# Constants generated in eight pieces, own keys by differences of values, heads' result split two at a time, gates loaded one pair ahead

## The chip, the core and the metric

The kernel runs on one core of a Trainium2 chip. The time is that of one launch on the device, in microseconds (us): the median of the runs of a version. The core's engines run side by side, each from its own queue of instructions in order, and wait for one another by semaphores: TensorE (PE in the profile, with its weight loads as PEld), VectorE (DVE), ScalarE (ACT), GpSimd (POOL) and SyncE (SP), which here issues the loads from device memory. Matmuls write to PSUM banks; DVE and ACT read them out.

## The reference

Two layers, each a mixer of sliding-window attention and a gated linear recurrence (HGRN2), merged by sigmoid gates, over 1024 tokens of width 1024, all in float32:

```python
for layer in range(DEPTH):                       # DEPTH 2
    h = rms_norm(x, norm_w[layer])
    q, k, v, z_attn, q_h, f_h, i_h, g_h, gate_attn, gate_hgrn = split(h @ w_in[layer])
    a = sliding_window_attention(rope(q), rope(k), v, sinks) * silu(z_attn)   # 8 heads of 64, 2 kv heads, window 128
    o = hgrn2_recurrence(silu(q_h), (1 - lb) * sigmoid(-f_h), i_h, log(lb + (1 - lb) * sigmoid(f_h)))
    b = rms(o) * hgrn_norm_w[layer] * silu(g_h)                                # 4 heads of 128
    x = x + (sigmoid(gate_attn) * (a @ w_up_attn[layer])
             + sigmoid(gate_hgrn) * (b @ w_up_hgrn[layer])) @ w_out[layer]
return rms_norm(x, final_norm_w)
```

A query attends to the keys of its own block of 128 up to itself and to those of the block before that lie in the window. `lb` comes from `lb_logits` by a softmax over the layers; rotary embedding needs the cosine and sine of position times frequency. These, some masks and `hnw` (`hgrn_norm_w`) are the kernel's constants.

## The kernel before

Each float32 product is three matmuls of rounded parts (`proj3`: high x high, high x low, low x high). A weight chunk is loaded raw (`wr`), its high part is cast by ACT (`whi` or `wh`, L128) and its low part is a subtraction on DVE (`wlo` or `wl`, L129). The raw chunks share two buffers, so a load starts only when the chunk two before it has been split. All SBUF slots, PSUM banks and buffers come from pools; a planner sets the order on each engine by priorities from the order of the code and by when buffers and inputs are free. SyncE takes the loads in its own order: one that waits for a buffer holds up the rest.

A layer goes through these stages:

- **Input projection of gates, q, k and v by pairs** (`pair_first`, `pair_rest`, 13 pairs): a pair of 128 columns goes through sums of weight blocks (`ws`, L277 to L281), split into `whi_s`/`wlo_s` and `whi_t`/`wlo_t` and half a chunk split into `wh`/`wl` (L285, L286), and five groups of 12 matmuls into the banks `pb` and `pc` (L291 to L293). DVE adds a bank to earlier parts (`pq`, L303), which frees it; ACT applies the sigmoid and sends the gate to memory (`gd`).
- **Constants** (layer 0): `constants()` runs whole behind pair 1. It loads the masks, makes `lb` and `oml`, the angles `ang` (L407, eight multiplications), their reduction (`nrn`, L410 to L423) and two sines (L426, L427). ACT holds one table of functions at a time, so the sines cost a load (L426) and a load back to the sigmoid's (L473). `tables()` behind pair 5 makes four tables `tab` of cosine and sine (memset by POOL, L436; DVE, L439 to L443), turns each by four PE transposes (`tt`, L447) and stores it.
- **z, attention, values**: attention runs block by block (8 blocks), with projections between. `scores` puts own keys and those of the block before into one tile of 128 columns (a column is either the one or the other), `softmax` makes `pr`, `turn` transposes it (`tp`, L721) and DVE multiplies it twice from PSUM (L724): by the mask of past keys, `side[:, 0]`, into `pT[:, 0]` and by that of own keys into `pT[:, 1]`. `values` (L733) multiplies these by the values `vn` of the block before and of its own into `av`.
- **HGRN heads**: `core(h)` for four heads in a stagger of 25 steps, with `filling()` between: the heads' projections, then `up_attn` (`pu_ua`; its result `u1` is copied by ACT, L800, and multiplied by the gate `ga`, L825). `finish_head` transposes a head's result (`tb`, L1020) and DVE writes it to half of `b` (L1021); `b` has two halves of the tokens (`a`) and two pairs of heads. Behind the last head, `split_act` casts the four parts on ACT (`b0h`, `b1h` in layers 0 and 1, L781) and subtracts on DVE (`b0l`, `b1l`, L782).
- **Up projection of HGRN**: for each pair `m` of eight column blocks `up_chunk` loads weights (`wr_uh`), `gate_in` loads two gates `u2` (shown as `u<-gd`, L806), PE makes `pu_uh`, DVE multiplies by the gate in place (L802), adds `u1` (L1080), and ACT and DVE split the sum into `mg` (L1082, L1083).
- **Output projection** with `w_out` (`wr_o`, `po`), and in layer 0 the loads of `x` for the next norm.

Of the kernel before, what the change touches and what calls it, by code (L numbers as in the profile page):

```python
# [10 lines left out]
F32 = mybir.dt.float32  # L11
# [27 lines left out]
def trunk_kernel(ctx, tc, x, positions, norm_w, w_in, attn_sinks, hgrn_norm_w, w_up_attn,  # L39
# [313 lines left out]

    tabs = [dp.tile([P, T], F32, name=f"tabs_{i}") for i in range(2)]

    def constants():

        ones = cp.tile([P, 32], F32, name="ones")
        G.memset(ones, 1.0)
        side = cp.tile([P, 2, P], F32, name="side")  # L360
        nc.sync.dma_start(side, c_side)
        upper = cp.tile([P, P], I32, name="upper")
        nc.sync.dma_start(upper, c_upper)
        never = cp.tile([P, 1], F32, name="never")
        G.memset(never, -1e30)
        mdiag = cp.tile([P, 32], F32, name="mdiag")
        nc.sync.dma_start(mdiag, c_diag)
        mlev = cp.tile([P, NLEV, 32], I32, name="mlev")
        nc.sync.dma_start(mlev, c_lev)
        freq = cp.tile([P, HALF], F32, name="freq")  # L370
        nc.sync.dma_start(freq, c_freq)
        posi = cp.tile([P, NB], I32, name="posi")
        nc.sync.dma_start(posi, positions.rearrange("o (b p) -> p (o b)", p=P))
        sink = cp.tile([P, DEPTH, NH], F32, name="sink")
        nc.sync.dma_start(sink, attn_sinks.rearrange("(o l) h -> o l h", o=1).broadcast_to([P, DEPTH, NH]))
        hnw = cp.tile([P, DEPTH], F32, name="hnw")
        nc.sync.dma_start(hnw, hgrn_norm_w.rearrange("l p -> p l"))
        lbl = cp.tile([P, DEPTH, NHG], F32, name="lbl")
        nc.sync.dma_start(lbl, lb_logits.rearrange("l (h p) -> p l h", p=P))


        lbm = cp.tile([P, NHG], F32, name="lbm")
        tc.keep_in_program_order(V.tensor_tensor(out=lbm, in0=lbl[:, 0], in1=lbl[:, 1], op=ALU.max))
        lbe = cp.tile([P, DEPTH, NHG], F32, name="lbe")
        for l in range(DEPTH):
            V.tensor_tensor(out=lbe[:, l], in0=lbl[:, l], in1=lbm, op=ALU.subtract)
        S.activation(lbe, lbe, AF.Exp)
        lbs = cp.tile([P, NHG], F32, name="lbs")
        V.tensor_tensor(out=lbs, in0=lbe[:, 0], in1=lbe[:, 1], op=ALU.add)
        V.reciprocal(lbs, lbs)  # L390
        lsm = cp.tile([P, DEPTH, NHG], F32, name="lsm")
        for l in range(DEPTH):
            V.tensor_tensor(out=lsm[:, l], in0=lbe[:, l], in1=lbs, op=ALU.mult)
        lb = cp.tile([P, DEPTH, NHG], F32, name="lb")
        V.tensor_tensor(out=lb[:, 0], in0=lsm[:, 0], in1=lsm[:, 0], op=ALU.subtract)
        lbc = cp.tile([P, NHG], F32, name="lbc")
        V.tensor_tensor(out=lbc, in0=lsm[:, 0], in1=lsm[:, 1], op=ALU.add)
        V.tensor_tensor(out=lb[:, 1], in0=lbc, in1=lsm[:, 0], op=ALU.subtract)
        oml = cp.tile([P, DEPTH, NHG], F32, name="oml")
        V.tensor_scalar(out=oml, in0=lb, scalar1=-1.0, scalar2=1.0, op0=ALU.mult, op1=ALU.add)  # L400


        posf = cp.tile([P, NB], F32, name="posf")
        tc.keep_in_program_order(V.tensor_copy(posf, posi))
        ang = cp.tile([P, NB, HALF], F32, name="ang")
        for b in range(NB):
            V.tensor_scalar(out=ang[:, b], in0=freq, scalar1=posf[:, b:b + 1], scalar2=None, op0=ALU.mult)  # L407
        nrn = cp.tile([P, NB, HALF], F32, name="nrn")
        big = 1.5 * 2.0 ** 23
        V.tensor_scalar(out=nrn, in0=ang, scalar1=1.0 / (2.0 * math.pi), scalar2=None, op0=ALU.mult)  # L410
        V.tensor_scalar(out=nrn, in0=nrn, scalar1=big, scalar2=None, op0=ALU.add)
        V.tensor_scalar(out=nrn, in0=nrn, scalar1=-big, scalar2=None, op0=ALU.add)
        rest = 2.0 * math.pi
        for bits in (2, 8, 8, 24):
            if bits == 24:
                c = float(np.float32(rest))
            else:
                e = math.floor(math.log2(rest))
                q = 2.0 ** (e - (7 if bits == 8 else 7))
                c = math.floor(rest / q) * q  # L420
            V.scalar_tensor_tensor(out=ang, in0=nrn, scalar=-c, in1=ang, op0=ALU.mult, op1=ALU.add)
            rest -= c
        V.tensor_scalar(out=ang, in0=ang, scalar1=3.1415925, scalar2=-3.1415925, op0=ALU.min, op1=ALU.max)  # L423
        sins = cp.tile([P, NB, HALF], F32, name="sins")

        S.activation(sins, ang, AF.Sin)  # L426
        S.activation(nrn, ang, AF.Sin, scale=0.5)  # L427
        V.tensor_tensor(out=nrn, in0=nrn, in1=nrn, op=ALU.mult)
        return ones, side, upper, never, mdiag, mlev, sink, hnw, lb, oml, sins, nrn

    def tables(sins, nrn):
        for i in range(2):
            for g in range(2):
                b = slice(4 * g, 4 * g + 4)
                t = hp.tile([P, 4, P], F32, tag="po", name=f"tab_{i}_{g}")
                G.memset(t, 1.0 - i)  # L436
# [19 lines left out]
    def first_chunk(L, m, slots):  # L456

        nm = f"p{L}_{m}"
        return (split_slot if slots else split_w)(load_chunk(w_in[L], pairs[m][0][0], nm), nm, [P, KT, P])


    for L in range(DEPTH):
# [135 lines left out]
        for m in range(NPAIR):  # L598
# [8 lines left out]
                    S.activation(tr[r][:, t0:t0 + 512], o[key], AF.Copy, scale=qkv[r][1])  # L607
            if m == 12:
                cosT, sinT = rotary()
            if L == 0 and m == 1:  # L610
                ones, side, upper, never, mdiag, mlev, sink, hnw, lb, oml, *angles = constants()
            elif L == 0 and m == 5:
                tables(*angles)
        for i, (part, nm) in enumerate(((hT.hi, "hi"), (hT.lo, "lo"))):
            for j in range(2):
                part[1][j] = slot([P, 2, 512], f"h{nm}_{L}_{j}", F32R)
# [25 lines left out]
        def z(j, w, groups):  # L642
# [4 lines left out]
                nc.scalar.dma_start(zd[:, j, t], d)  # L647
            colsA(w[0], w[1], hT, f"z{L}_{j}", use, groups)

        w = [chunk(wi, OZ + j * P, f"z{L}_{j}") for j in range(2)]  # L650
        stack(0)
        stack(1)
# [12 lines left out]
        z(2, w[2], [H0, H1])  # L665
        stack(5)
        z(3, w[3], [H0, H1])


        probs = {}  # L670
# [43 lines left out]
        def turn(b):  # L714
            pr, _ = probs[b]
            probs[b] = []
            for g in range(2):

                tp = bank([P, 2, 2, P], f"tp_{L}_{b}_{g}")
                for j in range(4):  # L720
                    PE.transpose(tp[:, j % 2, j // 2], pr[:, 4 * g + j], ident)  # L721
                pT = slot([P, 2, 4, P], f"pT_{L}_{b}_{g}")
                for pt in ([0, 1] if b else [1]):
                    V.tensor_tensor(out=pT[:, pt], in0=tp.rearrange("p r i q -> p (r i) q"),  # L724
                                    in1=side[:, pt].unsqueeze(1).broadcast_to([P, 4, P]), op=ALU.mult)
                probs[b].append(pT)

        def values(b):
            av = bank([P, 4, P], f"av_{L}_{b}")
            for g, pT in enumerate(probs.pop(b)):  # L730
                for pt in ([0, 1] if b else [1]):
                    for r in range(2):
                        PE.matmul(av[r * HD:(r + 1) * HD, 2 * g:2 * g + 2].rearrange("p h q -> p (h q)"),  # L733
                                  lhsT=vn[0][:, b if pt else b - 1, g * HD:(g + 1) * HD],
                                  rhs=pT[:, pt, 2 * r:2 * r + 2].rearrange("p h q -> p (h q)"),
                                  start=pt == 0 or b == 0, stop=pt == 1)
            d = hp.tile([P, 4, P], F32, tag="po", name=f"avo_{L}_{b}")
# [31 lines left out]
        for u in range(4):  # L769
            before(NB + u)  # L770
            (forget if u < 2 else query)(0, w[u // 2], [(H0, H1)[u % 2]])
            attend(NB + u)

        def split_act(src, nm):
            res = []
            for a in range(2):
                row = []
                for j in range(2):
                    hi = slot([P, 2, 512], f"{nm}h_{a}_{j}", F32R)
                    lo = slot([P, 2, 512], f"{nm}l_{a}_{j}", F32R)  # L780
                    S.copy(hi, src[a][j])  # L781
                    V.tensor_tensor(out=lo, in0=src[a][j], in1=hi.bitcast(F32), op=ALU.subtract)  # L782
                    row.append((hi, lo))
                res.append(row)
            return res


        def up_chunk(w, m, nm):
# [38 lines left out]


        bt = [[None] * 2 for _ in range(2)]

        scTs = [slot([P, NB, P], f"scT_{L}_{i}") for i in range(2)]
        for t in scTs:
# [2 lines left out]
        def core(h):  # L835
# [176 lines left out]
            def finish_head():  # L1012
                gs = slot([P, T], f"gg_{nm}")
                nc.sync.dma_start(gs, gd[(2 * KT + h) * P:(2 * KT + h + 1) * P])
                for a in range(2):
# [3 lines left out]
                    for j in range(4):  # L1019
                        PE.transpose(tp[:, j], ot[:, 4 * a + j], ident)  # L1020
                    V.scalar_tensor_tensor(out=bt[a][h // 2][:, h % 2], in0=tp.rearrange("p j q -> p (j q)"),  # L1021
                                           scalar=hnw[:, L:L + 1], in1=gs[:, a * 512:(a + 1) * 512],
                                           op0=ALU.mult, op1=ALU.mult)
            finish[h] = finish_head

        def gate_attn(asp):
# [38 lines left out]
        finish[done]()  # L1065
        for _ in fill:
            pass
        bsp = split_act(bt, f"b{L}")


        mg = [[None] * KT for _ in range(2)]
        for m in range(0, KT, 2):
            w = up_chunk(w_up_hgrn[L], m, f"uh{L}_{m}")
            u2 = [gate_in(KT + m + j, f"u2_{L}_{m + j}") for j in range(2)]
            for j in range(2):
                for a in range(2):
                    t = slice(a * 512, (a + 1) * 512)
# [94 lines left out]

def _constants():
    p = np.arange(P)
    past = p[:, None] > p[None, :]
    side = np.stack([past, ~past], axis=1).astype(np.float32)
    upper = (p[None, :] > p[:, None]).astype(np.int32)
    s, t = (p % 32)[:, None], np.arange(32)[None, :]
    diag = (s == t).astype(np.float32)
# [33 lines left out]
```

## Time and profile before

| | us |
|---|---|
| runs | 1458.06, 1456.96, 1456.90 |
| median | 1456.96 |
| the profiled execution | 1455.78 |
| its span | 1454.0 |
| PE, PEld busy | 1419.4, 1147.5 |
| DVE, ACT, POOL busy | 934.8, 676.9, 70.0 |

The granted TensorE clock was 0.998 over the span. 1.78 us of the profiled execution lie around its span. All stretches in the text are counted from the span's start. Rows of a timeline give the start, the length of the group, the engine, the line of the code, the operation, its output and inputs, and how many instructions stand in the row (x8); brackets give how long the engine had been idle and what ended the wait. Matmuls of 128x512 start 0.23 us apart when nothing holds them up, though one is shown as 0.39 us long.

### The profile page before, as it was taken

To read this page: it belongs to the slowest core of one execution; us is meant where nothing else is said; L and a number is where in the kernel's file an instruction comes from. 1 tells how busy PE (TensorE), PEld (TensorE's weight loads), DVE (VectorE), ACT (ScalarE), POOL (GpSimd) and SP (SyncE) were. 2 spreads that over 40 slices of the span, in tenths; PEclk is the share of its full clock that TensorE was granted. 3 is DMA by queue.
4 is the path that set the end of the run, shared out by engine and by line. 5 is a ranking of instruction groups with operands and counts; after the bars stand their busy time and mean duration, and the time that the engine had idled before them with its cause. 6 is when DMAs were issued, how large, how long until landed. Compare 5 with 4: busy or idle time off the path is not lost.

```text
span 1454.0 us, 21306 instructions
## 1 busy us (share of the span) xinstructions
PE 1419.4 (98%) x8252; PEld 1147.5 (79%) x8252; DVE 934.8 (64%) x1586; ACT 676.9 (47%) x1354; POOL 70.0 (5%) x77
## 2 busy tenths in 40 slices
PE   8999999999999999999999999999999999999997
PEld 7877778877777778778888878888787777887886
DVE  6856655655755889673657466666456578967643
ACT  8754332345574654422556332433467555443321
POOL 1100000220000001000000000003000000000000
PEclk9999999999999999999999999999999999999999
DMA  8433443464135654336554334436523366443431
GB/s 272 154 107 124 134 142 123 134 169 150 59 131 173 215 191 148 130 101 232 174 182 159 113 126 130 133 99 200 167 79 102 124 209 219 153 174 101 160 145 58
DMA packets 194277, 214.41 MB, mean 147 GB/s; under 512 B 12480, under 2 KB 142016, under 8 KB 194176
## 3 DMA queue, kind: packets, MB, share of 16 engines
q1 hardware_dynamic: 161152, 161.66, 34.9%
q10 hardware_dynamic: 31488, 46.15, 8.6%
q0 software_dynamic: 1536, 5.24, 0.9%
q8 instruction: 65, 1.06, 0.3%
q14 instruction: 36, 0.29, 0.1%
HBM read 145.65 MB, written 59.77 MB: 141 GB/s over the span
## 4 chain that ended last, share of the span: by engine, by line
PE 77%; DVE 8%; ACT 6%; DMA 6%; issue 2%; SPq 0%; ACTq 0%; DVEq 0%; POOL 0%
PE pb L291 4%; PE pb L292 4%; PE pb L293 4%; PE pg L263 3%; PE pg L265 3%; DMA wr<-in_w_in_dram 3%; PE pg L264 3%; PE pc L291 2%; PE pc L292 2%; PE pc L293 2%; PE pj_qh L139 2%; PE pj_qh L140 2%; PE av L733 2%; PE pj_qh L141 2%; PE pj_f L139 2%
## 5 line engine op out<-in xcount | busy, mean ns | idle before, releaser
L128 ACT CAST whi_s<-ws 128x1024 fp32r<-128x1024 f32 x26 | 27.4, 1053 | 128.8 <-DVE ws L278 118.1
L724 DVE TENSOR_TENSOR pT<-tp,side 128x512 f32<-128x512 f32 x60 | 39.1, 679 | 23.5 <-PE tp L721 23.5
L139 PE MATMUL pu_ua<-wh_a,wlo_ua 128*128 128x512 f32 x128 | 52.5, 410 | 0.0
L263 PE MATMUL pg<-hh,wlo_p 128*128 128x512 f32 (+1 forms) x128 | 47.6, 376 | 3.1 <-POOL wlo_p L129 1.5
L141 PE MATMUL pu_ua<-wh_a,whi_ua 128*128 128x512 f32 x128 | 50.5, 395 | 0.0
L1160 PE MATMUL po<-wlo_o,mg 128*128 128x512 f32 x128 | 49.9, 390 | 0.4 <-DVE wlo_o L129 0.4
L709 ACT ACTIVATE pr<-pr,mx 128x128 f32<-128x128 f32 x128 | 49.9, 395 | 0.8 <-ACT it L759 0.8
L140 PE MATMUL pu_ua<-wl_a,whi_ua 128*128 128x512 f32 x128 | 50.2, 392 | 0.0
L473 ACT ACTIVATE pq<-pq 128x512 f32<-128x512 f32 x60 | 37.7, 631 | 26.5 <-DVE pq L303 25.2
L1159 PE MATMUL po<-whi_o,mg 128*128 128x512 f32 x128 | 49.9, 390 | 0.0
L1161 PE MATMUL po<-whi_o,mg 128*128 128x512 f32 x128 | 49.6, 389 | 0.0
L694 DVE COPY_PREDICATED pr<-upper,sc 128x256 f32<-128x256 int32 x56 | 23.2, 442 | 40.7 <-ACT pr L693 40.7
L1082 ACT CAST mg<-u 128x512 fp32r<-128x512 f32 x32 | 19.5, 621 | 60.7 <-DVE u L1080 60.6
L264 PE MATMUL pg<-hl,whi_p 128*128 128x512 f32 (+1 forms) x128 | 46.8, 370 | 0.0
L265 PE MATMUL pg<-hh,whi_p 128*128 128x512 f32 (+1 forms) x128 | 46.7, 369 | 0.0
L277 DVE TENSOR_TENSOR ws<-wr 128x512 f32<-128x512 f32 x26 | 17.9, 689 | 41.9 <-DMA wr<-in_w_in_dram 41.9
L303 DVE TENSOR_TENSOR pq<-pb,p 128x512 f32<-128x512 f32 x40 | 27.6, 689 | 26.6 <-PE pb L293 26.6
L129 DVE TENSOR_TENSOR wlo_t<-ws,whi_t 128x1024 fp32r<-128x1024 f32 x26 | 31.8, 1224 | 18.1 <-ACT whi_t L128 18.0
L800 ACT COPY u<-pu_ua 128x512 f32<-128x512 f32 x32 | 18.8, 588 | 51.9 <-PE pu_ua L141 51.6
L291 PE MATMUL pb<-th,wlo_s 128*128 128x512 f32 x104 | 40.7, 391 | 2.0 <-DVE wlo_s L129 2.0
L291 PE MATMUL pc<-hh,wlo_t 128*128 128x512 f32 x104 | 41.5, 399 | 1.0 <-DVE pq L303 1.0
L291 PE MATMUL pb<-th,wl 128*128 128x512 f32 x104 | 41.1, 395 | 0.8 <-DVE pq L303 0.8
(394 smaller groups left out, 4478.5 us busy)
## 6 DMA issues: line engine op xcount, KB each, us to landing
wr<-in_w_in_dram SPq DMA_DIRECT2D x64, 512.0 KB
gd<-pq ACTq DMA_DIRECT2D x76, 256.0 KB
wr_p<-in_w_in_dram SPq DMA_DIRECT2D x26, 512.0 KB
fq<-fq ACTq DMA_DIRECT2D x48, 256.0 KB
x<-in_x_dram SPq DMA_DIRECT2D x16, 512.0 KB
ga<-gd SPq DMA_DIRECT2D x16, 512.0 KB
u<-gd SPq DMA_DIRECT2D x16, 512.0 KB
wr_o<-in_w_out_dram SPq DMA_DIRECT2D x16, 512.0 KB
```

Of the source, the lines that this page charges most:

```text
L139: PE.matmul(acc, lhsT=ll, rhs=rh, start=i == 0, stop=False)
L140: PE.matmul(acc, lhsT=lh, rhs=rl, start=False, stop=False)
L141: PE.matmul(acc, lhsT=lh, rhs=rh, start=False, stop=i == n - 1)
L263: PE.matmul(acc, lhsT=wl[:, k], rhs=h[:, t], start=k == 0, stop=False, skip_group_check=q > 0)
L264: PE.matmul(acc, lhsT=wh[:, k], rhs=l[:, t], start=False, stop=False, skip_group_check=q > 0)
L265: PE.matmul(acc, lhsT=wh[:, k], rhs=h[:, t], start=False, stop=k % 4 == 3, skip_group_check=q > 0)
L291: PE.matmul(acc, lhsT=wl[:, k], rhs=h, start=start and k == 0, stop=False, skip_group_check=not start)
L292: PE.matmul(acc, lhsT=wh[:, k], rhs=l, start=False, stop=False, skip_group_check=not start)
L293: PE.matmul(acc, lhsT=wh[:, k], rhs=h, start=False, stop=k == 3, skip_group_check=not start)
L709: S.activation(pr[:, h], pr[:, h], AF.Exp, bias=mx[:, h:h + 1], accum_out=sm[:, h:h + 1])
L1159: PE.matmul(accs[j], lhsT=ll, rhs=wh[:, i], start=k + i == 0, stop=False)
L1160: PE.matmul(accs[j], lhsT=lh, rhs=wl[:, i], start=False, stop=False)
```

## The change

**Constants.** `constants()` becomes a generator with eight `yield`s, and `tables` is its last part; it is advanced once behind each pair from pair 0 of layer 0 on. So masks come behind pair 0, `lb` behind pair 1, the angles behind pair 2, their reduction behind 3, the sines behind 4, and a table each behind 5 to 8. `side` holds one mask.

**Own keys by differences.** Since a column of `tp` holds either a past or an own key, `pT[:, 0]` is now a plain copy of all columns by ACT, multiplied by the values of the block before, and `pT[:, 1]`, the own keys' columns as before, is multiplied by `vd`, the difference of own and earlier values. Number and size of the matmuls stay.

**Heads.** `split_act` goes; `finish_head` splits both halves behind each odd head by `split_slot`.

**Gates.** `u2` of the next pair are loaded in the step of this pair, behind its weights.

```diff
     def constants():
...
-        side = cp.tile([P, 2, P], F32, name="side")
+        side = cp.tile([P, P], F32, name="side")
...
+        made.update(ones=ones, side=side, upper=upper, never=never, mdiag=mdiag, mlev=mlev, sink=sink, hnw=hnw)
+        yield
...
+        made.update(lb=lb, oml=oml)
+        yield
...
             V.tensor_scalar(out=ang[:, b], in0=freq, scalar1=posf[:, b:b + 1], scalar2=None, op0=ALU.mult)
+        yield
         nrn = cp.tile([P, NB, HALF], F32, name="nrn")
...
             rest -= c
+        yield
         V.tensor_scalar(out=ang, in0=ang, scalar1=3.1415925, scalar2=-3.1415925, op0=ALU.min, op1=ALU.max)
...
-        return ones, side, upper, never, mdiag, mlev, sink, hnw, lb, oml, sins, nrn
-
-    def tables(sins, nrn):
         for i in range(2):
             for g in range(2):
+                yield
                 b = slice(4 * g, 4 * g + 4)
...
-            if L == 0 and m == 1:
-                ones, side, upper, never, mdiag, mlev, sink, hnw, lb, oml, *angles = constants()
-            elif L == 0 and m == 5:
-                tables(*angles)
+            next(consts, None)
...
+        vd = slot([P, NB - 1, P], f"vd_{L}")
+        V.tensor_tensor(out=vd, in0=vn[0][:, 1:], in1=vn[0][:, :NB - 1], op=ALU.subtract)
...
-                for pt in ([0, 1] if b else [1]):
-                    V.tensor_tensor(out=pT[:, pt], in0=tp.rearrange("p r i q -> p (r i) q"),
-                                    in1=side[:, pt].unsqueeze(1).broadcast_to([P, 4, P]), op=ALU.mult)
+                whole = tp.rearrange("p r i q -> p (r i) q")
+                if b:
+                    S.copy(pT[:, 0], whole)
+                V.tensor_tensor(out=pT[:, 1], in0=whole, in1=side.unsqueeze(1).broadcast_to([P, 4, P]), op=ALU.mult)
...
-                                  lhsT=vn[0][:, b if pt else b - 1, g * HD:(g + 1) * HD],
+                                  lhsT=(vd if b and pt else vn[0])[:, b - 1 if b else 0, g * HD:(g + 1) * HD],
...
-        def split_act(src, nm):
...
+        bsp = [[], []]
...
+                    if h % 2:
+                        bsp[a].append(split_slot(bt[a][h // 2], f"b{L}_{a}_{h // 2}", [P, 2, 512]))
...
-        bsp = split_act(bt, f"b{L}")
...
+        u2s = []
         for m in range(0, KT, 2):
             w = up_chunk(w_up_hgrn[L], m, f"uh{L}_{m}")
-            u2 = [gate_in(KT + m + j, f"u2_{L}_{m + j}") for j in range(2)]
+            u2s += [gate_in(KT + c, f"u2_{L}_{c}") for c in range(len(u2s), min(m + 4, KT))]
+            u2 = u2s[m:m + 2]
```

How it moves instructions is shown at three places. The first is DVE in layer 0, between the raw weights of pair 3 and of pair 4 (in the names `_2_`, `_3_` are pairs). Before, at the angles:

```order
L277 TENSOR_TENSOR ws_3_0_1410<-wr_3_1_1408 128x512
L407 TENSOR_SCALAR ang<-freq,posf 128x8 x8
L303 TENSOR_TENSOR pq_2_22_1331<-pc_2_1334,p_0_2_351 128x512
L410 TENSOR_SCALAR nrn<-ang 128x64
L278 TENSOR_TENSOR ws_3_0_1410<-ws_3_0_1410,wr_3_0_1406 128x512
```

and, 11 rows further on, at `wl` of pair 3:

```order
L423 TENSOR_SCALAR ang<-ang 128x64
L129 TENSOR_TENSOR wlo_3_t<-ws_3_1_1411,whi_3_t 128x1024
L303 TENSOR_TENSOR pq_2_21_1332<-pb_2_1333,p_0_2_351 128x512
L428 TENSOR_TENSOR nrn<-nrn 128x64
L303 TENSOR_TENSOR pq_3_12_1428<-pb_3_1431,p_0_2_351 128x512
L303 TENSOR_TENSOR pq_3_22_1429<-pc_3_1432,p_0_2_351 128x512
L286 TENSOR_TENSOR wl_3_1425<-wr_3_1_1408,wh_3_1424 128x512
```

With the change both stand together:

```order
L303 TENSOR_TENSOR pq_2_12_1306<-pc_2_1310,pq_2_12_1306 128x512
L303 TENSOR_TENSOR pq_2_21_1308<-pb_2_1309,p_0_2_351 128x512
L412 CAST posf<-posi 128x8
L415 TENSOR_SCALAR ang<-freq,posf 128x8 x8
L129 TENSOR_TENSOR wlo_3_t<-ws_3_1_1398,whi_3_t 128x1024
L286 TENSOR_TENSOR wl_3_1412<-wr_3_1_1395,wh_3_1411 128x512
L303 TENSOR_TENSOR pq_3_12_1415<-pb_3_1418,p_0_2_351 128x512
```

The angles come behind all of pair 2's `pq`, and `wl` of pair 3 ahead of pair 3's first `pq`. On ACT the load for the sine moves likewise behind pair 3's `wh` (L285).

The second place is DVE behind the last head of layer 0 (`tb_3` are its transposes); before:

```order
L1021 SCALAR_TENSOR_TENSOR b_1_1_5324<-tb_3_1_5472,hnw,gg_3_5464 128x512
L782 TENSOR_TENSOR b0l_0_5527<-b_0_0_4677,b0h_0_5526 128x1024
L825 TENSOR_TENSOR u_0_6_5403<-u_0_6_5403,ga_6_5520 128x1024
L825 TENSOR_TENSOR u_0_7_5404<-u_0_7_5404,ga_7_5523 128x1024
L782 TENSOR_TENSOR b0l_1_5531<-b_0_1_5317,b0h_1_5530 128x1024
L782 TENSOR_TENSOR b0l_0_5535<-b_1_0_4684,b0h_0_5534 128x1024
L782 TENSOR_TENSOR b0l_1_5539<-b_1_1_5324,b0h_1_5538 128x1024
```

and with the change:

```order
L1022 SCALAR_TENSOR_TENSOR b_1_1_5334<-tb_3_1_5486,hnw,gg_3_5474 128x512
L337 TENSOR_TENSOR wl_b_0_1_5483<-b_0_1_5327,wh_b_0_1_5482 128x1024
L337 TENSOR_TENSOR wl_b_1_1_5493<-b_1_1_5334,wh_b_1_1_5492 128x1024
L129 TENSOR_TENSOR wlo_uh_2_5633<-wr_uh_2_5630,whi_uh_2_5632 128x1024
L825 TENSOR_TENSOR u_0_6_5413<-u_0_6_5413,ga_6_5538 128x1024
```

Two subtractions are left there, ahead of the gated `u1`; the other two stand among the steps of heads 2 and 3.

The third is SyncE's queue at the up projection of layer 0 (`u_0_4` is gate 4); before:

```order
L806 DMA u_0_3_5632<-gd_138 128x1024
L1150 DMA wr_o_0_0_0_5908<-in_w_out_dram 128x2x512
L1150 DMA wr_o_0_0_2_5938<-in_w_out_dram 128x2x512
L806 DMA u_0_4_5712<-gd_138 128x1024
L806 DMA u_0_5_5714<-gd_138 128x1024
L1150 DMA wr_o_0_0_4_5968<-in_w_out_dram 128x2x512
```

and with the change:

```order
L806 DMA u_0_3_5556<-gd_138 128x1024
L790 DMA wr_uh_6_5794<-in_w_up_hgrn_dram 128x4x256
L1154 DMA wr_o_0_0_0_5910<-in_w_out_dram 128x2x512
L806 DMA u_0_4_5636<-gd_138 128x1024
L806 DMA u_0_5_5638<-gd_138 128x1024
L1154 DMA wr_o_0_0_2_5940<-in_w_out_dram 128x2x512
```

Gates 4 and 5 stand ahead of the second `w_out` load, and each later pair of gates one `w_out` load earlier.

More of the change, by code (lines that the diff above doesn't have):

```diff
@@ L354, in trunk_kernel @@
     tabs = [dp.tile([P, T], F32, name=f"tabs_{i}") for i in range(2)]
+    made = {}
     def constants():
@@ L459, in first_chunk @@
         return (split_slot if slots else split_w)(load_chunk(w_in[L], pairs[m][0][0], nm), nm, [P, KT, P])
+    consts = constants()
     for L in range(DEPTH):
@@ L648, in z @@
             colsA(w[0], w[1], hT, f"z{L}_{j}", use, groups)
+        ones, side, upper, never, mdiag, mlev, sink, hnw, lb, oml = (
+            made[n] for n in "ones side upper never mdiag mlev sink hnw lb oml".split())
         w = [chunk(wi, OZ + j * P, f"z{L}_{j}") for j in range(2)]
@@ L772, in trunk_kernel @@
             attend(NB + u)
-        def split_act(src, nm):
[L775 to L785, printed above, removed]
         def up_chunk(w, m, nm):
@@ L1174, in _constants @@
     p = np.arange(P)
-    past = p[:, None] > p[None, :]
-    side = np.stack([past, ~past], axis=1).astype(np.float32)
+    side = (p[:, None] <= p[None, :]).astype(np.float32)
     upper = (p[None, :] > p[:, None]).astype(np.int32)
```

## The prediction

> **What bounds the kernel now.** I read the page's busy times and chain first. The four rows are busy time of three engines, then the chain of work that ended last.
>
> ```profile
> PE 1419.4 (98%) x8252; PEld 1147.5 (79%) x8252; DVE 934.8 (64%) x1586; ACT 676.9 (47%) x1354; POOL 70.0 (5%) x77
> PE 77%; DVE 8%; ACT 6%; DMA 6%; issue 2%; SPq 0%; ACTq 0%; DVEq 0%; POOL 0%
> ```
>
> TensorE (PE) is the bound: 98% busy, and no edit removes a matmul. VectorE (DVE) has 519 us of slack over the span and ScalarE (ACT) 777 us, so moving work between them pays only where PE waits. What the change can win is therefore PE's waits. The view of PE's waits names them; columns are total us, times, longest.
>
> ```profile
> PE pb L291 <- DVE wlo_s L129: 2.0, 1, 2.0
> PE tt L447 <- DVE tab L440: 1.2, 1, 1.2
> PE pu_uh L139 <- DVE u L802: 1.1, 2, 0.7
> PE pc L291 <- DVE pq L303: 1.0, 2, 0.7
> PE pu_uh L139 <- ACT b1h L781: 1.0, 1, 1.0
> PE pu_uh L139 <- ACT b0h L781: 0.9, 1, 0.9
> PE pu_uh L140 <- DVE b1l L782: 0.2, 1, 0.2
> PE pu_uh L140 <- DVE b0l L782: 0.2, 1, 0.2
> ```
>
> These eight rows are 7.6 us, and all stand where the diff edits. A wait is less than the PE time lost by it: the last matmul before it is modelled as ending later than the next could have started, and the first one after it runs longer. So where I can, I take the gap between starts.
>
> **Constants in pieces.** Layer 0's pairs 2 and 6 carry all of the old cost. The rows are DVE, then ACT, then DVE, then PE, in order of time.
>
> ```profile
> 132.08 1.16 DVE L407 TENSOR_SCALAR ang<-freq,posf 128x8 f32<-128x8 f32 x8
> 133.15 0.68 DVE L303 TENSOR_TENSOR pq<-pc,p 128x512 f32<-128x512 f32 x1
> 139.10 1.28 ACT L426 ACT_TABLE_LOAD   x1
> 140.82 1.28 ACT L473 ACT_TABLE_LOAD   x1
> 143.72 0.62 ACT L285 CAST wh<-wr 128x512 fp32r<-128x512 f32 x1 [0.45 <-ACT pq L473]
> 145.75 0.68 DVE L286 TENSOR_TENSOR wl<-wr,wh 128x512 fp32r<-128x512 f32 x1
> 150.25 0.69 DVE L277 TENSOR_TENSOR ws<-wr 128x512 f32<-128x512 f32 x1 [1.69 <-DMA wr<-in_w_in_dram]
> 152.65 0.39 PE L292 MATMUL pb<-tl,wh 128*128 128x512 f32 x1
> 152.88 0.39 PE L293 MATMUL pb<-th,wh 128*128 128x512 f32 x1
> 155.25 0.50 PE L291 MATMUL pb<-th,wlo_s 128*128 128x512 f32 x1 [1.99 <-DVE wlo_s L129]
> ```
>
> First, the eight `ang` multiplies (1.16 us) stand ahead of `pq`, which empties the bank that `pc` needs. The new order puts `pq` ahead of `posf` and `ang`, behind which now stands `wlo_3_t`, needed later. The wait of 0.7 of the 1.0 us goes; with the slower first matmul 0.9 us.
>
> Second, `wl` (145.75) is the last reader of pair 3's raw weights; only then can pair 4's load start, which lands at 150.2. `wl` was late because ACT cast `wh` at 143.72, behind the sine's two table loads, and then stood in DVE behind a `pq` that waited for PE. In the new order `wh` and `wl` come before both. Without the two loads (2.56) `wh` ends near 141.8, `wl` near 142.5, and nothing but `wl` holds the buffer: the load lands some 2.8 us earlier, near 147.4. The gap lost is 155.25 - 152.88 - 0.23 (the step from 152.65 to 152.88) = 2.14 us, and would go whole if all 2.8 came through. DVE's steps between load and `wlo_s` are many and mixed with `pq`s that wait for PE, so I take 1.6; bounds 0.8 and 2.2.
>
> Third, pair 6 (182.7 to 201.4), beside a plain pair before it and the same length in layer 1, which has no constants. Columns: length, then busy us of PE, PEld, DVE, ACT, POOL.
>
> ```profile
> 169.10:182.70 13.60, 13.60 (x61) 11.02 (x60) 8.88 (x12) 4.53 (x6) 0.53 (x1) 1.00 0.41 131
> 182.70:201.40 18.70, 16.68 (x82) 13.10 (x81) 10.46 (x28) 6.77 (x10) 1.58 (x3) 1.00 0.48 155
> 890.00:903.60 13.60, 13.60 (x61) 11.06 (x60) 8.71 (x13) 4.53 (x6) 0.00 (x0) 1.00 0.42 136
> ```
>
> Pair 6 takes 5.1 us more than its neighbour, 2.0 of them idle PE; the rest is the tables' transposes, which move but stay. The four tables come one a pair now (pairs 6 to 9), so PE has a whole pair in which DVE fills the next. I take the 2.0 idle less 0.1 for one more switch between transposes and projections: 1.9, bounds 0.8 (if a `pq` behind table work is still late, as one was) and 2.4. The smaller `side` load is hidden. Constants: -0.9 - 1.6 - 1.9 = -4.4 us.
>
> **Heads' result two at a time.** The split of heads 0 and 1 now runs when head 1 is done, that of 2 and 3 alone at the end. Rows: ACT, DVE, PE at the end, then DVE between head 1 and the end.
>
> ```profile
> 601.05 1.06 ACT L781 CAST b0h<-b 128x1024 fp32r<-128x1024 f32 x1 [1.07 <-DVE b L1021]
> 604.39 2.00 ACT L781 CAST b0h<-b 128x1024 fp32r<-128x1024 f32 x2
> 602.67 2.35 DVE L825 TENSOR_TENSOR u<-u,ga 128x1024 f32<-128x1024 f32 x2
> 604.15 0.40 PE L139 MATMUL pu_uh<-b0h,wlo_uh 128*128 128x512 f32 x1
> 605.49 0.50 PE L139 MATMUL pu_uh<-b0h,wlo_uh 128*128 128x512 f32 x1 [0.94 <-ACT b0h L781]
> 606.21 0.50 PE L140 MATMUL pu_uh<-b0l,whi_uh 128*128 128x512 f32 x1 [0.22 <-DVE b0l L782]
> 586.17 0.29 DVE L991 COPY R<-kv 128x128 f32<-128x128 f32 x1 [5.12 <-PE kv L987]
> ```
>
> The two gaps lose 605.49 - 604.15 - 0.23 = 1.11 and 606.21 - 605.49 - 0.23 = 0.49, with 0.1 in the next matmul 1.7 us; layer 1's waits are as long, so 3.4 in all. Two casts and two subtractions fewer stand at the end, and `u*ga` (2.35) behind them: the last cast ends near 603.1 and the last subtraction near 604.4, both before PE reaches those halves (604.2 for the first cast, 606.9 for the second). The displaced copies of `pu_ua` free their bank near 604.6, wanted at 605.5: next in line, 0.9 us clear. I take 3.3 (bounds 2 and 3.5). The early split adds 2 x 1.22 to a DVE that is full there, and this is absorbed by the 5.12 idle at 586.17.
>
> **Own keys by differences.** In 14 blocks, two multiplications each (28) leave DVE, and ACT gets 28 copies of 128x512 out of PSUM; the DVE multiplication for own keys now waits for the copy of the same tile. One subtraction per layer (128x896) joins DVE after `ql`. The groups give the prices; a row of the timeline shows two multiplications; the windows are layer 0's attention and ACT's fullest 8 us in it.
>
> ```profile
> L724 DVE TENSOR_TENSOR pT<-tp,side 128x512 f32<-128x512 f32 x60 | 39.1, 679 | 23.5 <-PE tp L721 23.5
> L800 ACT COPY u<-pu_ua 128x512 f32<-128x512 f32 x32 | 18.8, 588 | 51.9 <-PE pu_ua L141 51.6
> 415.98 1.29 DVE L724 TENSOR_TENSOR pT<-tp,side 128x512 f32<-128x512 f32 x2 [2.52 <-PE tp L721]
> 344.00:440.00 96.00, 96.00 (x549) 74.32 (x549) 60.46 (x131) 63.44 (x204) 1.84 (x2) 1.00 0.28 94
> 416.00:424.00 8.00, 8.00 (x44) 5.45 (x43) 6.55 (x15) 7.50 (x23) 0.00 (x0) 1.00 0.17 62
> ```
>
> DVE loses 28 x 0.68 = 19 us, ACT gains 28 x 0.59 = 16.5. PE is full throughout (96.00 of 96.00), so DVE's relief is worth nothing here. ACT goes from 63.4 to about 71.7 of 96 per layer. In 416-424 it would need 7.50 + 1.18 = 8.7 of 8, so it falls 0.7 us behind; the new order puts 11 to 38 matmuls (0.23 each, so over 2.5 us) between the transposes and `av` of blocks 5 and 6, and block 7's `av` follows eight or more `av` and transposes, where copy plus multiplication (1.3) fit. The subtraction stands where DVE waited for ACT. I take 0; bounds -1 (fewer switches between `av` and projections) and +2.2.
>
> The upper bound is the two readers of a tile going one behind the other with PE bare. The row of two multiplications is 1.29. Copy, hand-over and multiplication are 0.59 + 0.1 + 0.68 = 1.37; the 0.1 is an estimate from the split's rows, where the first of two casts ends near 605.4 and PE starts at 605.49. That is 0.08 more, 28 times. The Trainium skill ("PSUM — Partial Sum Buffer", PSUM bank collisions raise a hardware error) states that two engines may not touch one bank in the same partitions at once, reads included, and must be kept apart by a semaphore. By that rule a copy and a multiplication can't overlap, so the sum would hold this +2.2 wherever no other PE work covers it; no row of before shows ACT and DVE reading one `tp`.
>
> **Gates one pair ahead.** The chain's piece, SyncE's issue and DVE's wait:
>
> ```profile
> 618.23 11.07 SPq L1150 DMA_DIRECT2D wr_o<-in_w_out_dram  x2
> 629.39 5.09 DMA u<-gd
> 634.58 1.29 DVE L802 TENSOR_TENSOR u<-pu_uh,u 128x512 f32<-128x512 f32 x2 [3.71 <-DMA u<-gd]
> ```
>
> The gate loads 4 and 5 stood in SyncE's queue behind the second `wr_o`, which waits till 629 for its buffer. Now they stand ahead of it: issued near 618.7, landed by 623.8 at 5.09 each, and DVE wants them from 630.9 (3.71 before 634.58). PE's 1.1 us of waits (both layers) go; with 0.2 a time for the slower start, as at 605.49 and 606.21, 1.5. Gates 6 and 7 take the old place, one pair early, and land at 634.5 for a use one pair (48 matmuls, 10.9 us) after 630.9. The fourth `wr_o` now stands behind four `x` loads: 0, since those need no buffer that the `wr_o` of before didn't outwait; at most +0.7, the longest that a late gate cost PE. Gates: -1.5.
>
> **Sum.** -4.4 + 0 - 3.3 - 1.5 = -9.2. I give back 0.7, since the loads paced by buffers keep their landing times: -8.5. The profiled execution is 1455.78 us (span 1454.0), 1.18 below the runs' median 1456.96; 1456.96 - 8.5 = 1448.5.
>
> **The rivals.**
> - ACT late in attention. For: it is at 7.50 of 8 before 1.18 more. Against: PE's cover there. If `av` waits 1.2 us in each of 14 blocks, +16.8: 1465. It decides at (8.5 + 2.9) / 14 = 0.8 us per block; between 0.4 and 0.8 it is about level with before.
> - The constants' stalls move. For: `wr` paces DVE even in plain pairs. Then only 1.2 of 4.4 is won: 1451.7.
> - The two readers in a row, bare: 1448.5 + 2.2 = 1450.7.
> - The early split delays heads 2 and 3. For: DVE is full there. Up to 2.4 us a layer reach PE before 581: 1448.5 + 4.8 = 1453.3.
>
> ```profile
> 540.00:560.00 20.00, 19.77 (x281) 15.40 (x279) 19.10 (x44) 9.04 (x25) 3.55 (x4) 1.00 0.42 159
> ```
>
> **How the numbers follow.** 0.2%, 2.9 us, is what can be told from no change. Forecast 0.52; constants move 0.15; readers bare 0.07; heads delayed 0.10 (0.04 faster, 0.06 same); ACT late 0.16, half same and half slower. Faster 0.78, same 0.14, slower 0.08. The range: below, all upper gains (5.5 + 1 + 3.5 + 1.7 = 11.7) give 1445; above, 1456 takes in every rival but ACT late at its worst.
>
> **What would show it.** Right: the waits on `wlo_s`, on `tab` at `tt`, on the heads' split and on `u` at `pu_uh` are gone from PE's list; pair 6 near 14.5 us; attention still 96 of 96. Wrong: PE waiting for ACT copies at `av`; new waits at `l` or `lv` between 545 and 581; `wr` still landing near 150.

## The result and the profile after

The changed kernel took 1445.86 us (median of 4 runs, 1443.37 to 1446.89) against 1457.51 us before (4 runs, 1456.90 to 1459.88). The ratio is 0.9915, with a 95% interval of 0.9897 to 0.9932: 12.4 us less by the ratio, 9.9 to 15.0. The forecast was 1448.5, 8.5 less. The profiled execution is 1446.19 us with a span of 1444.4, against 1455.78 and 1454.0.

The page after the change, busy time and chain:

```profile
PE 1415.8 (98%) x8252; PEld 1149.4 (80%) x8252; DVE 922.1 (64%) x1560; ACT 691.1 (48%) x1382; POOL 68.6 (5%) x77
PE 78%; DVE 7%; ACT 6%; DMA 5%; issue 2%; SPq 0%; ACTq 0%; DVEq 0%
```

TensorE issues the same 8252 instructions and is still the bound. DVE fell by 12.7 us and ACT rose by 14.2. The view of TensorE's waits (total us, times, longest) lacks all eight rows that the prediction listed. Two others stand in both views, here each before and then after: the waits on `pq` at `pb` stay, and those on `R` at the matmul `l` of the heads have grown.

```profile
PE pb L291 <- DVE pq L303: 1.6, 5, 0.8
PE pb L291 <- DVE pq L303: 1.7, 7, 0.3
PE l L967 <- DVE R L869: 0.5, 2, 0.2
PE l L968 <- DVE R L870: 1.3, 2, 0.7
```

Where the time came from is read by taking one TensorE matmul after another, the same ones in both traces, and subtracting the start before from the start after. The growth of that difference over a stretch is what the stretch gained (minus) or lost, in us; stretches are named by their time in the trace of before, and the columns to the right are the experiments below.

| stretch | after | const | keys | split | gates | split_gates | whole_av | keys_dve | late |
|---|---|---|---|---|---|---|---|---|---|
| 131-170, constants in pairs 2, 3 | -2.7 | -2.8 | 0 | -0.1 | -0.2 | -0.4 | +1.5 | -0.3 | -2.7 |
| 170-290, tables | -2.4 | -2.1 | -0.5 | -0.1 | -0.3 | -0.3 | -0.6 | 0 | -2.2 |
| 387-401 and 1085-1111, block 2 | -2.0 | 0 | -2.0 | 0 | 0 | 0 | -0.9 | 0 | -2.0 |
| 567-582 and 1278-1292, `l` | +1.0 | 0 | +0.1 | +1.0 | +0.1 | +1.0 | 0 | 0 | +0.1 |
| 604-612 and 1314-1322, end of heads | -3.6 | 0 | 0 | -3.6 | 0 | -3.6 | 0 | 0 | -3.6 |
| 612-640 and 1322-1350, gates | -1.7 | -0.1 | 0 | +3.1 | -1.7 | -1.7 | +0.2 | +0.1 | -1.7 |

These six rows sum to -11.4 for the changed kernel. Not in the table are stretches in which kernels that differ in nothing there scatter by a microsecond or two, above all z (290 to 350), where TensorE waits for loads; the last section says what most of this is. In the row of the tables the kernels that leave the constants alone stand between 0 and -0.6, so up to 0.6 of the gain there can be scatter too.

The constants in the changed kernel, rows of DVE, ACT and PE in order of time, beside those that the prediction quoted:

```profile
142.52 0.69 DVE L286 TENSOR_TENSOR wl<-wr,wh 128x512 fp32r<-128x512 f32 x1
147.19 0.69 DVE L277 TENSOR_TENSOR ws<-wr 128x512 f32<-128x512 f32 x1 [1.09 <-DMA wr<-in_w_in_dram]
150.99 1.22 DVE L129 TENSOR_TENSOR wlo_s<-ws,whi_s 128x1024 fp32r<-128x1024 f32 x1
146.56 1.28 ACT L483 ACT_TABLE_LOAD   x1
136.45 0.50 PE L291 MATMUL pb<-th,wl 128*128 128x512 f32 x1 [0.27 <-DVE pq L303]
180.30:195.00 14.70, 14.47 (x66) 11.50 (x65) 8.65 (x16) 5.11 (x7) 0.53 (x1) 1.00 0.46 142
```

`wl` stands at 142.52 where it stood at 145.75, pair 4's load lands 3.1 us sooner, `wlo_s` is done by 152.2, and the wait of 2.0 us is gone whole. The table load back from the sines now comes behind `wl` and holds nobody up. At 136.45 a wait of 0.27 us is new, one `pq` further on: half of what the first step won. The last row is a window over pair 6: 14.7 us long, 0.2 of them without a matmul against 2.0.

### The profile page after: what moved, and what is told of

It reads as the page before. It is cut to its first block, busy times and chain, and to the rows that moved or that the text cites. A ratio compares the mean times of both kernels' runs of the same rounds, so it can differ in the third digit from the quotient of the medians.

```text
span 1444.4 us, 21317 instructions
## 1 busy us (share of the span) xinstructions
PE 1415.8 (98%) x8252; PEld 1149.4 (80%) x8252; DVE 922.1 (64%) x1560; ACT 691.1 (48%) x1382; POOL 68.6 (5%) x77
## 4 chain that ended last, share of the span: by engine, by line
PE 78%; DVE 7%; ACT 6%; DMA 5%; issue 2%; SPq 0%; ACTq 0%; DVEq 0%
PE pb L291 4%; PE pb L293 4%; PE pb L292 4%; PE pg L263 3%; PE pg L265 3%; PE pc L291 3%; PE pg L264 3%; PE pc L293 2%; PE pc L292 2%; PE pj_qh L139 2%; PE pj_qh L141 2%; PE pj_qh L140 2%; PE av L746 2%; PE pj_f L139 2%; PE pj_f L140 2%; PE pj_f L141 2%
## 5 line engine op out<-in xcount | busy, mean ns | idle before, releaser
L139 PE MATMUL pu_uh<-wh_b,wlo_uh 128*128 128x512 f32 x128 | 49.8, 389 | 0.0
L140 PE MATMUL pu_uh<-wl_b,whi_uh 128*128 128x512 f32 x128 | 49.8, 389 | 0.0
L141 PE MATMUL pu_uh<-wh_b,whi_uh 128*128 128x512 f32 x128 | 49.8, 389 | 0.0
L263 PE MATMUL pg<-hh,wl_p 128*128 128x512 f32 (+1 forms) x112 | 41.2, 369 | 1.8 <-DVE wl_p L337 1.2
```

Of the source, the lines that this page charges most:

```text
L139: PE.matmul(acc, lhsT=ll, rhs=rh, start=i == 0, stop=False)
L140: PE.matmul(acc, lhsT=lh, rhs=rl, start=False, stop=False)
L141: PE.matmul(acc, lhsT=lh, rhs=rh, start=False, stop=i == n - 1)
L263: PE.matmul(acc, lhsT=wl[:, k], rhs=h[:, t], start=k == 0, stop=False, skip_group_check=q > 0)
```

## The experiments

Ratios are to the kernel before, timed beside each set of experiments (medians 1456.98 us for the four parts, 1456.73 for the rest), with 95% intervals.

**The four parts alone.** Each is the kernel before with one part of the diff.

```diff
 const:  constants() as a generator, next(consts, None) behind each pair; side keeps two masks
 keys:   + vd = vn[:, 1:] - vn[:, :NB - 1];  S.copy(pT[:, 0], whole);  lhsT = vd for own keys
 split:  - bsp = split_act(bt, ...)   + split_slot behind each odd head
 gates:  + u2s, up to four gates ahead
```

> The kernel before with the constants in pieces alone (two masks still in side). Theory, each part takes away its own waits of TensorE and the parts add up: 5 us less (the changed kernel's trace is 5.1 us ahead at 300 us), the waits on wlo_s and on tab at tt gone, everything from 310 us on as before. Rival, the forecast's bound for this part: 4.4 us less. Rival, the stalls only move once the other parts are missing: under 2 us less.

Measured: 1451.64 us, ratio 0.9957 (0.9946 to 0.9969), 6.3 us less (4.5 to 7.9). The trace gives 4.9 in the constants' stretches, and 0.1 or nothing in the other rows of the table. The first theory holds; it does not need the other parts.

> The kernel before with own keys by differences alone, copies on ScalarE. The forecast had 0. Theory after the result: 2.0 us less, 1.0 in each layer, all of it within 6 us around the values of block 2, where the planner no longer puts the scores of block 5 between them. Rival, the bare chain of two readers: up to 2.2 us more. Rival, the relief of VectorE: nothing at block 2, small gains in every block.

Measured: 1455.14 us, ratio 0.9987 (0.9978 to 0.9996), 1.9 us less (0.6 to 3.2), all of it at block 2, once in each layer. TensorE's rows there, before, from the first values of block 2 to the scores behind the last ones:

```profile
387.88 0.65 PE L733 MATMUL av<-pT,vn 128*64 128x256 f32 x4
388.46 0.50 PE L685 MATMUL sc<-ks,qs 128*128 128x256 f32 x2
388.90 0.65 PE L733 MATMUL av<-pT,vn 128*64 128x256 f32 x4
389.48 0.38 PE L689 MATMUL sc<-ks,qs 128*128 128x256 f32 x1
389.79 0.65 PE L733 MATMUL av<-pT,vn 128*64 128x256 f32 x4
390.37 0.39 PE L689 MATMUL sc<-ks,qs 128*128 128x256 f32 x1
390.60 0.28 PE L685 MATMUL sc<-ks,qs 128*128 128x256 f32 x1
390.81 0.65 PE L733 MATMUL av<-pT,vn 128*64 128x256 f32 x4
391.39 0.39 PE L685 MATMUL sc<-ks,qs 128*128 128x256 f32 x1
391.62 0.39 PE L689 MATMUL sc<-ks,qs 128*128 128x256 f32 x2
391.85 0.40 PE L685 MATMUL sc<-ks,qs 128*128 128x256 f32 x2
```

and in the kernel with the keys alone:

```profile
385.56 0.65 PE L737 MATMUL av<-pT,vn 128*64 128x256 f32 x4
386.04 0.60 PE L737 MATMUL av<-pT,vd 128*64 128x256 f32 x4
386.48 0.60 PE L737 MATMUL av<-pT,vn 128*64 128x256 f32 x4
386.91 0.60 PE L737 MATMUL av<-pT,vd 128*64 128x256 f32 x4
387.44 0.50 PE L688 MATMUL sc<-ks,qs 128*128 128x256 f32 x2
```

Groups of `av` that stand together start 0.43 to 0.48 us apart. Alone, each takes 0.58 until the scores start, and two scores between them take 0.44 (from 388.46, and again from 390.37) in place of 0.23 (from 391.62 to 391.85). All rows touch, and neither kernel shows TensorE waiting there, so only the starts show the loss.

> The kernel before with the heads' result split two heads at a time alone. Theory: 3.5 us less at the end of the heads (1.8 a layer) and 0.5 a layer given back at the matmul l of head 2 or 3, which waits for VectorE's R behind the two early subtractions: 2.5 us less in all. Rival, the forecast: 3.3 less, the early subtractions absorbed by VectorE's idle time. Rival: the wait at l comes from another part of the change, then it is 0.2 a layer here as before.

Measured: 1457.33 us, ratio 0.9999 (0.9990 to 1.0009): nothing, against 2.5 less by the theory. The end of the heads did gain 3.6 and the wait at `l` did grow by 1.0. What the theory lacked is a new wait among the up projection's matmuls in each layer, for gate 2, and a longer one for gate 4, 3.1 us in all. Layer 0's waits, then SyncE's issue of gates 2 and 3 in the kernel before, the issues with the split, and DVE's row at gate 2:

```profile
PE pu_uh L139 <- DVE u L788: 1.8, 2, 1.0
PE l L954 <- DVE R L856: 0.7, 1, 0.7
610.11 0.93 SPq L806 DMA_DIRECT2D u<-gd  x2
614.99 0.38 SPq L1138 DMA_DIRECT2D wr_o<-in_w_out_dram  x1
615.46 0.89 SPq L792 DMA_DIRECT2D u<-gd  x2
620.81 1.29 DVE L788 TENSOR_TENSOR u<-pu_uh,u 128x512 f32<-128x512 f32 x2 [3.27 <-PE pu_uh L141]
```

The planner put gates 2 and 3 behind the first `w_out` load, which waits for its buffer till 615; before, they went out at 610.11. DVE's row names TensorE as what it waited for; but 615.46 and the 5.09 us that such a load takes in the prediction's chain make 620.6, and in the trace its last part lands at 620.69, so it is the load. Without the fourth part, the third lengthens the very waits that the fourth removes.

> The kernel before with the gates loaded one pair ahead alone. Theory: 1.7 us less (0.95 and 0.75 at the wait for gate 4 in the two layers), nothing else. Rival, the loads pushed back matter: the wait on wlo_o near 700 us grows by 0.3, so 1.4 less. Rival: without the split, VectorE is late itself at gate 4, and less than 0.8 is won.

Measured: 1455.15 us, ratio 0.9982 (0.9972 to 0.9992), 2.6 us less (1.2 to 4.1). The trace has 1.7 at the gates; the wait on `wlo_o` near 700 us, with its cast, rose from 0.4 to 1.2 us. Before, then two rows with the gates, then the kernel with the constants alone:

```profile
PE po L1160 <- DVE wlo_o L129: 0.4, 1, 0.4
PE po L1162 <- DVE wlo_o L129: 0.8, 1, 0.8
PE po L1161 <- ACT whi_o L128: 0.4, 1, 0.4
PE po L1169 <- DVE wlo_o L129: 0.7, 1, 0.7
```

This would fit the first rival, that the loads pushed back matter. But the kernel with the constants alone, which leaves these loads where they were, waits 0.7 there too, and the changed kernel, which pushes them back, waits 0.7 without the cast's 0.4. The rival is not shown.

**Split and gates together.**

> The kernel before with split and gates together. Theory: they depend on each other. The split alone took 1.8 us a layer from the end of the heads and lost it at two waits for gates (at 620 and 632 us), whose loads come at their old time; with the gates ahead those waits go, so 3.5 + 1.7 - 1.0 at the matmul l = 4.2 us less, against 0 and 1.8 for the parts alone. Rival, parts add: 1.5 to 2 us less. Rival: the early subtractions are what the split loses, then 2.8 less at most and the waits at l are more than 0.5 a layer.

Measured: 1451.82 us, ratio 0.9963 (0.9950 to 0.9976), 5.4 us less (3.5 to 7.3), where the parts alone gave 0.1 and 2.6. By the table -3.6, -1.7 and +1.0: 4.3. The waits at the gates are gone; between 530 and 700 us there remain those for the last head and at `l`:

```profile
PE tb L1007 <- DVE tab L998: 0.7, 1, 0.7
PE l L954 <- DVE R L856: 0.7, 1, 0.7
```

**What the keys gained by.** Two kernels take order and arithmetic apart. The first keeps the arithmetic of before and pins the order at block 2 (likewise in `proj3` for block 7 of `i`, which follows):

```diff
+                        if b == 2:
+                            tc.keep_in_program_order(one)   # each matmul of values(2)
...
+                        if b == 5:
+                            tc.keep_in_program_order(one)   # the first of each two in scores(5)
```

> The kernel before with one thing changed, the order on TensorE at block 2: the four instructions of its values, the scores of block 5 and the first projections of block 7 of i are kept in the order of the code, so the values stand together as with the change; no copy, no difference. Theory, the order alone makes the gain of the keys: 1.0 us less in each layer, 2.0 in all. Rival, the arithmetic (ScalarE's copies, a VectorE that is free sooner) makes it: 0.

Measured: 1455.65 us, ratio 0.9992 (0.9981 to 1.0002), which the times can't tell from no change. The table has 0.9, half of the theory. One row holds all sixteen:

```profile
387.69 2.36 PE L736 MATMUL av<-pT,vn 128*64 128x256 f32 x16
389.97 0.50 PE L686 MATMUL sc<-ks,qs 128*128 128x256 f32 x2
386.86 2.48 DVE L727 TENSOR_TENSOR pT<-tp,side 128x512 f32<-128x512 f32 x4
```

From the first `av` to the scores pass 2.28 us, against 1.88 with the keys. DVE makes its four `pT` until 389.34, while these `av` run, so they take them as they come: in the trace the second, third and last four `av` start at 388.19, 388.79 and 389.39, each 0.05 us behind the end of a `pT`. The view of waits names none of this. Where the `pT` are made in time, the same kernel's sixteen `av` take 1.87 us, as at block 1 of layer 1, whose last `pT` is done at 1086.93:

```profile
1087.86 1.95 PE L736 MATMUL av<-pT,vn 128*64 128x256 f32 x16
1089.73 0.50 PE L686 MATMUL sc<-ks,qs 128*128 128x256 f32 x2
```

The second computes by differences, but copies on VectorE:

```diff
-                    S.copy(pT[:, 0], whole)
+                    V.tensor_copy(pT[:, 0], whole)
```

> Own keys by differences alone, but with the copies on VectorE in place of ScalarE; the planner then keeps the old order, with the scores of block 5 between the values of block 2. Theory, order: 0, within 0.5 us of before, and the stretch at block 2 as long as before. Rival, arithmetic: 2 us less as with the copies on ScalarE.

Measured: 1457.61 us, ratio 1.0003 (0.9995 to 1.0011); 0 at block 2. Differences as such are worth nothing. About half of the gain is order, shown by the pinned kernel's trace. The other half is 0.5 us a layer, and 0.40 of it is the pinned kernel's longer stay at `av` (2.28 against 1.88). With the keys alone this stay is short because ACT and DVE have made all four `pT` by 385.78, before the second four `av` start at 386.04:

```profile
382.68 1.06 ACT L728 COPY pT<-tp 128x512 f32<-128x512 f32 x2
384.50 1.28 DVE L729 TENSOR_TENSOR pT<-tp,side 128x512 f32<-128x512 f32 x2
```

These rows show it; no kernel changed this alone.

**The early split later.** In the changed kernel the split of heads 0 and 1 is moved behind head 2, where DVE waits 5 us for `kv`.

```diff
-                    if h % 2:
-                        bsp[a].append(split_slot(bt[a][h // 2], f"b{L}_{a}_{h // 2}", [P, 2, 512]))
+                    if h > 1:
+                        bsp[a].append(split_slot(bt[a][h - 2], f"b{L}_{a}_{h - 2}", [P, 2, 512]))
```

> The changed kernel with the split of heads 0 and 1 behind head 2 in place of head 1, where VectorE then sits idle for 5 us. Theory, the early subtractions delay R of head 2's l: the wait at l falls from 0.7 to 0.2 us in both layers, 1.0 us less than the changed kernel. Rival, the wait at l comes from elsewhere: no change. Rival, moved to the idle time they delay kv's copy: new waits near 585 us, no gain.

Measured: 1442.50 us (1441.70 to 1443.38), ratio 0.9900 (0.9886 to 0.9914), the fastest of all. Waits, then DVE's rows behind head 2:

```profile
PE l L968 <- DVE R L870: 0.5, 2, 0.2
571.74 1.22 DVE L337 TENSOR_TENSOR wl_b<-b,wh_b 128x1024 fp32r<-128x1024 f32 x1 [0.38 <-ACT wh_b L336]
573.67 1.23 DVE L337 TENSOR_TENSOR wl_b<-b,wh_b 128x1024 fp32r<-128x1024 f32 x1
578.31 0.29 DVE L992 COPY R<-kv 128x128 f32<-128x128 f32 x1 [2.27 <-PE kv L988]
```

The wait at `l` is back at 0.2, and DVE is still idle for 2.3 us before `kv`: it had room for both subtractions. The table gives 0.9 us less than the changed kernel; the intervals of the two ratios overlap, so the times alone don't separate them.

## Why the prediction was right, and where its steps were off

Sign, range and the two largest terms held, but the time lies only 0.9 us above the range's lower end of 1445: the sum was 3 to 4 us short. The terms give 2.9 of this: 2.0 from the own keys, 0.7 each from the constants and the give-back, 0.5 from heads and gates, less the 1.0 lost at `l`.

- **Constants**, -4.4 forecast, -5.1 in the trace. `wl` and the load came when forecast (142.5 and 147.4 against 142.52 and 147.19), but I allowed 1.6 of the 2.14 us gap, and all of it went: the `pq`s between load and `wlo_s` were not late. The angles' step was right in kind, and half of it came back at the next `pq`. The tables gave 2.4 rather than 1.9, a difference within the scatter of that row. Pair 6 took 14.7 us where 14.5 was forecast.
- **Heads**, -3.3 forecast, -3.6 at their end. But the step "absorbed by the 5.12 idle at 586.17" failed: the idle time lies behind `l`, and `R` of `l` stands between. The rival that the early split delays the heads was true beside the forecast, 1.0 us of its 4.8, and so was one sign of being wrong, the new wait at `l` near 571 us; the split behind head 2 shows it.
- **Gates**, -1.5 forecast, -1.7. The terms for split and gates were added as if each stood alone. Their sum is right only because both are in the change, which is luck: the split alone is worth 0.
- **Own keys**, 0 forecast, -2.0. The step "PE is full throughout (96.00 of 96.00), so DVE's relief is worth nothing here" failed. Full by busy time was not full speed: at block 2 TensorE changed seven times between values and scores. The bound of -1 had named fewer switches, between `av` and projections, and 2.0 lies beyond it; close to half of the 2.0 goes with DVE no longer making all four `pT`, which I had put at nothing. ACT was late for nobody, as forecast, and the two readers of a tile cost nothing: with the keys alone TensorE waits for nothing between 340 and 440.
- **Give-back**, +0.7 forecast. No such loss is seen.

The two readers go one behind the other, and that costs less than I allowed. In none of the 28 pairs does DVE's multiplication start before ACT's copy has ended; in eight it starts 0.03 us behind it, where I had put 0.1, so that copy and multiplication together take 1.29 to 1.31, what two multiplications took (1.29). In four DVE stands idle for the copy:

```profile
DVE pT L738 <- ACT pT L737: 10.1, 4, 3.7
```

The 2.2 us did not come; other work of TensorE covered these waits. The Trainium skill ("PSUM — Partial Sum Buffer", PSUM bank collisions raise a hardware error) says that two engines that use one bank are to be kept apart by a semaphore. The order of these pairs agrees with it; what would happen without the semaphore no run here shows.

## What to carry to other kernels

Parts of a change that share a queue can't be costed one by one: ask what each does to the wait that the other removes, and which load the planner moves behind which. Where the bound engine shows no idle time, look at the starts of its instructions group by group: forms that alternate cost time that no wait shows. Before work is called absorbed by another engine's idle time, check that nothing between the work and the idle time is awaited. A wait that grows by less than a microsecond is first looked up in kernels that leave its place alone.

## What the runs showed of the hardware

In six of the ten profiled executions the granted clock fell to half once between 30 and 1430 us, for 3.4 us; seven matmuls in a row then start 0.43 us apart in place of 0.23, 1.4 to 1.6 us in all. In the changed kernel's trace it was here (length, busy us, then after POOL's count the granted clock):

```profile
331.00:334.50 3.50, 3.50 (x10) 2.73 (x9) 2.65 (x3) 2.42 (x3) 0.00 (x0) 0.52 0.75 224
```

So this profiled execution is about 1.5 us longer for it, and without it the traces' difference is 11 us, near that of the medians. The pinned kernel's +1.5 at 131 to 170 in the table is such a fall, from 156.7 us. It is also most of the scatter at z: the three kernels with a fall there (after, const, gates) lose 0.6 to 0.8 us from 290 to 350, the other six gain 0.7 to 1.1.

All six falls come right behind a long wait of TensorE. In the 3.41 us ahead of each TensorE was busy for only 1.36 to 1.88 us. Two of these waits, with the gates alone (fall from 308.3) and in the pinned kernel:

```profile
308.13 0.67 PE L139 MATMUL pj_z<-hh,wlo_z 128*128 128x512 f32 x1 [2.05 <-DVE wlo_z L129]
155.17 0.50 PE L292 MATMUL pb<-th,wlo_s 128*128 128x512 f32 x1 [2.07 <-DVE wlo_s L129]
```

The second is the wait on `wlo_s` that the change takes away. Not every such wait is followed by a fall: before's 1.99 at 155.25 is not, nor one of 1.74 at 303.75 in the kernel with the late split. What decides was not tried.

All ten traces end in a fall, and ahead of 20 us five of them, before's among them, have one of 3.4 or 6.8 us. This is before's early one (same columns):

```profile
15.00:18.00 3.00, 3.00 (x16) 3.00 (x16) 2.25 (x6) 2.85 (x7) 0.00 (x0) 0.50 0.97 336
```

It doesn't bear on the table: counted from the span's start, the same matmuls near 131 us lie within 0.7 us of each other in all ten traces, and not sorted by who has it.
